# Seven quarter products in place of eight for most of an MLP's first product, in a two-layer fp32 decoder trunk on one core

## The chip, the core and the metric

The kernel runs on one core of a Trainium2 chip. A core has a matrix engine (TensorE, PE in the profile; its weight loads are PEld), VectorE (DVE), ScalarE (ACT), GpSimd (POOL) and SyncE (SP), each with an instruction queue of its own that is worked through in order, and 16 DMA engines. The metric is the device time of one execution in microseconds (us); lower is better.

## The reference

Two layers, each with a mixer and an MLP, work on 512 tokens of 1024 features, all in float32. The change touches the MLP alone:

```python
D_FF = 4 * D_MODEL      # 4096, with D_MODEL 1024, SEQ 512, DEPTH 2
h = rms_norm(x, g_pre_mlp[l]) * (1 + sc_mlp) + sh_mlp
f = jnp.square(jax.nn.relu(h @ w_ff1[l].astype(h.dtype))) @ w_ff2[l].astype(h.dtype)
x = x + gt_mlp * rms_norm(f, g_post_mlp[l])
```

`sc_mlp`, `sh_mlp` and `gt_mlp` are adaLN values: parts of `c_act @ w_ada[l] + b_ada[l]`, a product of one vector with a 1024 x 6144 matrix for each layer.

## The kernel before, in words

Activations lie with features on the 128 partitions and the 512 tokens along the free axis, so the MLP's `h` is 8 tiles of 128 x 512, its hidden layer 32 such tiles, and its result 8.

**Precision.** The matrix engine works on fp32r, so every operand is split into a high part (a cast) and a low part (what the cast lost). A product block is three passes, high by high, high by low and low by high (`passes`, L173 to L179, the three matmul lines L177, L178 and L179). An activation pair lies in one `slot`.

**Weights.** A block of 128 output features by 1024 inputs (512 KB) comes by one DMA on SP's queue into `raw` (RAW = 4 buffers); ACT casts the high part (L169) and POOL subtracts for the low part (L170). The halves go to `whi` and `wlo`, two buffers each. A tile of a first or second product with such a block (`gemm`) is 8 times 3 matmuls of 128 x 512.

**The MLP** (L763 to L803), for each layer: `wff1` tiles 0 to 6 in two token halves of 256 (`gemm_parts`; their weights were preloaded while the mixer ended), tiles 7 to 15 at 512 tokens; then `wff2` over the first half of the hidden layer (8 result tiles, two weight blocks each); then `wff1` tiles 16 to 31; then `wff2` over the third quarter (8 tiles, one block each, added to `y` on DVE at L798); the last quarter is done in `finish`, in token halves, which also adds the residual, computes norms and starts what follows. Six of its eight blocks are split ahead of it into free slots (KF = 6). After each `wff1` tile `f_out` (L764 to L769) squares the relu: ACT relu (L766), DVE product into PSUM (L767), ACT cast to the high part (L768), DVE subtraction to the low part (L769).

**Columns.** 56 of the adaLN values' 128-row columns, most of them of layer 1, are worked out during layer 0's MLP. `ada_col` loads a 512 KB block by SP's queue into `adr` (ADR = 3 buffers) and reduces it against a broadcast vector on DVE (L272, 128 x 1024, both inputs in SBUF). `some(n)` puts n of them behind a tile: before, 1 behind each full `wff1` tile and 2 behind each `wff2` tile.

**Order.** The tile scheduler orders each engine's queue by program order and priorities; weight work stands earlier in program order than its use (`high_priority`). `mm` has three PSUM banks; `cv`, `ax` and `cx` are further banks.

Of the kernel before, what the change touches and what calls it, by code (L numbers as in the profile page):

```python
# [53 lines left out]
def trunk(ctx, tc, xT, vecs, bg, cst, ccol, crow, wadn, wadt, win, win0, wqkv, wgate, wout, wff1, wff2, yT):  # L54
# [103 lines left out]
    def wblock(src, alloc=None, lo_eng=None, pri=None):  # L158
        n = src.shape[-1]
        with tc.high_priority(offset=WPRI if pri is None else pri):  # L160
            flat = lambda t: t.rearrange("p a b -> p (a b)")
            raw = wpool.tile([P, n], F32, name="raw", tag="raw", bufs=RAW)
            if alloc is not None:
                hi, lo = flat(alloc())[:, 0:n], flat(alloc())[:, 0:n]
            else:
                hi = wpool.tile([P, n], F32, name="whi", tag="whi", bufs=WHI)
                lo = wpool.tile([P, n], F32, name="wlo", tag="wlo", bufs=WLO)
# [5 lines left out]
    def passes(out, w, col, pair, first, last, ts=slice(0, T)):  # L173
# [589 lines left out]
    def mlp(l, hp, pre):  # L763
        def f_out(o, pr, ts):  # L764
# [136 lines left out]
```

## Time and profile before

| what | before |
|---|---|
| runs (three) | 1609.31, 1610.56, 1612.74 us, median 1610.56 |
| the profiled execution | 1608.05 us, of which the span from the first to the last instruction is 1606.3 |
| PE busy | 1537.6 us (96%) |
| DVE, POOL, ACT busy | 878.1 (55%), 798.5 (50%), 688.6 us (43%) |
| chain that ended last | PE 78%, DVE 6%, ACT 2%, POOL 1% |
| mean granted TensorE clock | 0.989 |

Layer 0's MLP lies between about 480 and 830 us of the span, layer 1's between about 1245 and 1606. An engine's busy share is an average over stages; the rows below are of single stages.

### The profile page before, as it was taken

What the parts mean: (1) busy time and instruction counts of PE and PEld (TensorE: products, weight loads), DVE (VectorE), ACT (ScalarE), POOL (GpSimd) and SP (SyncE); (2) the same over time, 40 slices, a digit from 0 to 9 for tenths busy, and PEclk for the clock granted to TensorE, in tenths of its full rate; (3) what the DMA queues carried; (4) which work ended last, traced back from release to release, by engine and by line L of the source; (5) the groups of instructions that cost most, each with busy time, mean ns of one, the idle gap of its engine ahead of it and who ended that gap; (6) DMA issues with size and microseconds to landing.
All of it is one profiled execution on the core that took longest, in us unless ns stands there. A gap on an engine that the chain in (4) does not pass through costs nothing.

```text
span 1606.3 us, 21229 instructions
## 1 busy us (share of the span) xinstructions
PE 1537.6 (96%) x8020; PEld 1255.5 (78%) x8020; DVE 878.1 (55%) x1761; ACT 688.6 (43%) x1168; POOL 798.5 (50%) x488
## 2 busy tenths in 40 slices
PE   4899998999999999999999999999999999999997
PEld 3577665677998888888899777676899888888887
DVE  6399999843164432346747999997326320012114
ACT  3345563453454322332453665544355432233242
POOL 0166662256744444445962877434674444444462
PEclk9999999999999999999999999999999999999999
DMA  8514332413412555556730222220242233222331
GB/s 309 194 53 138 116 131 104 144 53 92 145 53 94 191 187 197 174 194 218 255 116 8 73 79 67 91 79 27 84 141 65 80 95 102 92 92 92 96 127 53
DMA packets 56270, 188.91 MB, mean 118 GB/s; under 512 B 6376, under 2 KB 8552, under 8 KB 56168
## 3 DMA queue, kind: packets, MB, share of 16 engines
q1 hardware_dynamic: 56168, 187.56, 35.2%
q8 instruction: 63, 1.03, 0.3%
q14 instruction: 39, 0.32, 0.1%
HBM read 185.44 MB, written 2.10 MB: 117 GB/s over the span
## 4 chain that ended last, share of the span: by engine, by line
PE 78%; DVE 6%; ACT 2%; POOL 1%; issue 1%; DMA 0%; POOLq 0%; ACTq 0%; DVEq 0%
PE ps_mm L177 23%; PE ps_mm L179 23%; PE ps_mm L178 23%; DVE ps_cv L429 3%; PE ps_mm L672 2%; PE ps_mm L660 2%; PE ps_ax L316 1%; PE ps_ax L245 1%; POOL wlo L170 1%; ACT whi L169 1%; PE ps_ax L578 1%; PE ps_ax L647 0%; DVE csb L490 0%; PE ps_ax L342 0%; PE ps_ax L701 0%
## 5 line engine op out<-in xcount | busy, mean ns | idle before, releaser
L170 POOL TENSOR_TENSOR wlo<-raw,whi 128x1024 fp32r<-128x1024 f32 (+1 forms) x216 | 498.8, 2311 | 565.1 <-ACT whi L169 547.0
L177 PE MATMUL ps_mm<-slot,whi 128*128 128x512 f32 (+1 forms) x1632 | 621.9, 382 | 8.1 <-ACT slot L155 4.9
L179 PE MATMUL ps_mm<-slot,wlo 128*128 128x512 f32 (+1 forms) x1632 | 622.1, 382 | 5.0 <-POOL wlo L170 4.8
L178 PE MATMUL ps_mm<-slot,whi 128*128 128x512 f32 (+1 forms) x1632 | 621.7, 381 | 0.0
L169 ACT CAST whi<-raw 128x1024 fp32r<-128x1024 f32 (+1 forms) x216 | 216.4, 1002 | 498.9 <-PE ps_mm L178 357.7
L177 PEld LDWEIGHTS ps_mm<-slot,whi 128*128 128x128 f32 x1632 | 307.3, 188 | 78.9 <-ACT slot L155 5.6
L179 PEld LDWEIGHTS ps_mm<-slot,wlo 128*128 128x128 f32 x1632 | 307.6, 188 | 73.8 <-issue 6.3
L178 PEld LDWEIGHTS ps_mm<-slot,whi 128*128 128x128 f32 x1632 | 308.0, 189 | 65.6 <-issue 3.8
L429 DVE SCALAR_TENSOR_TENSOR ps_cv<-slot,vv,ps_cv 128x512 f32<-128x512 f32 x480 | 332.9, 747 | 1.5
L767 DVE TENSOR_TENSOR ps_mm<-rl,ps_mm 128x512 f32<-128x512 f32 (+1 forms) x78 | 46.7, 599 | 280.6 <-ACT rl L766 280.5
L177 PE MATMUL ps_mm<-slot 128*128 128x256 f32 (+1 forms) x568 | 158.5, 292 | 14.5 <-DVE slot L769 7.4
L178 PE MATMUL ps_mm<-slot 128*128 128x256 f32 (+1 forms) x568 | 163.2, 290 | 0.3 <-POOL slot L355 0.3
L179 PE MATMUL ps_mm<-slot 128*128 128x256 f32 (+1 forms) x568 | 162.6, 289 | 0.0
L177 PEld LDWEIGHTS ps_mm<-slot 128*128 128x128 f32 x568 | 105.3, 190 | 19.9 <-ACT slot L357 8.4
L179 PEld LDWEIGHTS ps_mm<-slot 128*128 128x128 f32 x568 | 107.8, 190 | 2.2 <-issue 0.8
L178 PEld LDWEIGHTS ps_mm<-slot 128*128 128x128 f32 x568 | 107.6, 190 | 1.9 <-POOL slot L355 0.5
L170 POOL TENSOR_TENSOR slot<-raw,slot 128x1024 fp32r<-128x1024 f32 x34 | 85.2, 2527 | 14.4 <-issue 12.7
L272 DVE CUSTOM_DVE_ANT_0 adr<-adr,cbc,ini 128x1024 f32<-128x1024 f32 x40 | 66.0, 1659 | 23.3 <-DMA adr<-in_wadt 23.3
L147 POOL TENSOR_TENSOR small<-small,mhalf 128x4 f32<-128x4 f32 (+1 forms) x38 | 34.6, 911 | 81.3 <-DVE small L146 76.6
L769 DVE TENSOR_TENSOR slot<-ps_mm,slot 128x512 fp32r<-128x512 f32 (+1 forms) x78 | 46.4, 595 | 38.2 <-ACT slot L768 37.9
L530 POOL TENSOR_TENSOR xa<-xa,s 128x512 f32<-128x512 f32 x48 | 61.9, 1289 | 5.1 <-ACT s L529 1.9
L768 ACT CAST slot<-ps_mm 128x512 fp32r<-128x512 f32 (+1 forms) x78 | 39.8, 510 | 45.9 <-DVE ps_mm L767 45.9
(201 smaller groups left out, 1570.5 us busy)
## 6 DMA issues: line engine op xcount, KB each, us to landing
raw<-in_wff SPq DMA_DIRECT2D x138, 512.0 KB, 3.5
raw<-in_win SPq DMA_DIRECT2D x58, 512.0 KB, 3.3
adr<-in_wadt SPq DMA_DIRECT2D x56, 512.0 KB, 4.5
raw<-in_wout SPq DMA_DIRECT2D x36, 512.0 KB, 3.5
adr<-in_wadn SPq DMA_DIRECT2D x28, 512.0 KB, 4.2
raw<-in_wqkv SPq DMA_DIRECT2D x24, 256.0 KB, 2.6
slot<-in_wadt SPq DMA_DIRECT2D x8, 512.0 KB, 5.1
raw<-in_win SPq DMA_DIRECT2D x8, 384.0 KB, 7.1
```

The costliest lines, as they stand in the source:

```text
L147: pool.tensor_tensor(y, u, mhalf[:, 0:n], op=ALU.pow)
L169: act.copy(out=r32(hi), in_=raw)
L170: (lo_eng or pool).tensor_tensor(r32(lo), raw, hi, op=ALU.subtract)
L177: pe.matmul(out, whi, xh, start=first, stop=False)
L178: pe.matmul(out, whi, xl, start=False, stop=False)
L179: mark[0] = pe.matmul(out, wlo, xh, start=False, stop=last)
L272: red = dve.tensor_tensor_reduce(raw, raw, cbc, scale, 0.0 if one else ini, ALU.mult, ALU.add, m)
L429: dve.scalar_tensor_tensor(acc, at[i][:, k:k + T], w, acc, op0=ALU.mult, op1=ALU.add)
L530: pool.tensor_tensor(acc, acc, tk, op=ALU.add)
L767: dve.tensor_tensor(o, rl[:, ts], o, op=ALU.mult)
L768: act.copy(out=r32(pr[:, 0, ts]), in_=o)
L769: last[0] = dve.tensor_tensor(r32(pr[:, 1, ts]), o, pr[:, 0, ts], op=ALU.subtract)
```

## The change

In the first product the 32 output tiles are worked in four groups of eight. Tiles 0 to 7 stay as they were (NB = 8 in halves, where there were 7). Tiles 8 to 31 are worked in twelve pairs for each layer. A pair's 256 outputs, 1024 inputs and 512 tokens are cut into halves each, and the eight products of quarters become seven (`pair_out`: w1 to w7 are the seven combinations of weight quarters, `hp`, `ta` and `tb` the activations' combinations). A quarter product is 4 times 3 matmuls of 256 tokens, so a pair is 84 matmuls of 128 x 256 where it was 48 of 128 x 512. The activation combinations `ta` and `tb` are made once for each layer (`quarters`). The weight combinations are made for each pair: `s1` and `s2p` in PSUM (ACT copy, two DVE operations), `s3` on POOL, `s4` on DVE, seven high casts on ACT, five low subtractions on POOL and two on DVE, all 128 x 512. Results are summed on the way out of PSUM: `p1` (an ACT copy), `u2`, `q5` and three more additions on DVE, all 128 x 256, and four `f_out` of 128 x 256 instead of two of 128 x 512. Weights share one tag of four buffers.

Group g's hidden tiles feed one block of `wff2` (8 tiles, each followed by a copy to `y` or an addition); the last group's block stays in `finish`. `some` now puts 2 columns behind each `wff2` tile of group 0, 3 in group 1 and 2 in group 2; none stand behind `wff1` tiles.

```diff
-    NB = 7
+    NB = 8
-    WHI = 2
-    WLO = 2
+    WBUF = 4
...
+        def quarters():
+            for k in range(4):
+                b1, b2 = s2(), s2()
+                dve.tensor_tensor(b1, hp[k][:, 0, :], hp[k][:, 1, :], op=ALU.add)
+                dve.tensor_tensor(b2, hp[4 + k][:, 0, :], hp[4 + k][:, 1, :], op=ALU.add)
+                pa, pb = bank("ax"), bank("cx")
+                dve.tensor_tensor(pa[:, A], b1[:, B], b1[:, A], op=ALU.subtract)
+                dve.tensor_tensor(pa[:, B], b2[:, B], b1[:, B], op=ALU.subtract)
+                dve.tensor_tensor(pb[:, A], b2[:, B], pa[:, A], op=ALU.subtract)
+                dve.tensor_tensor(pb[:, B], b2[:, A], pb[:, A], op=ALU.subtract)
...
+        def pair_out(m, pm, pm1):
...
+                s1, s2p = bank("ax"), bank("cx")
+                act.copy(out=s1, in_=a21)
+                w1 = wq(a11, pool)
+                dve.tensor_tensor(s1, a22, s1, op=ALU.add)
+                dve.tensor_tensor(s2p, s1, a11, op=ALU.subtract)
+                w6 = wq(s2p, dve)
+                w2 = wq(a12, pool)
+                w5 = wq(s1, dve)
+                s3, s4 = s2(), s2()
+                pool.tensor_tensor(s3, a11, a21, op=ALU.subtract)
+                w7 = wq(s3, pool)
+                dve.tensor_tensor(s4, a12, s2p, op=ALU.subtract)
+                w3 = wq(s4, pool)
+                w4 = wq(a22, pool)
...
+            bx, ba, bb, bc = (bank(t)[:, 0:T // 2] for t in ("mm", "cv", "mm", "mm"))
+            p1, u2, q5 = sqt(), sqt(), sqt()
+            prod(bx, w1, hp[0:4], h0)
+            act.copy(out=p1, in_=bx)
+            prod(ba, w6, tb, h0)
+            dve.tensor_tensor(u2, ba, p1, op=ALU.add)
+            prod(bx, w2, hp[4:8], h0, True)
+            f_out(bx, pm, h0)
+            prod(bb, w5, ta, h0)
+            dve.tensor_tensor(q5, bb, u2, op=ALU.add)
+            prod(bc, w7, ta, h1)
+            dve.tensor_tensor(ba, bc, q5, op=ALU.add)
+            f_out(ba, pm1, h1)
+            prod(bb, w3, hp[4:8], h1, True)
...
+            prod(bc, w4, tb, h1, True)
...
-        for hf in range(2):
+        for g in range(4):
...
+                for u in range(4):
+                    fp += [slot(), slot()]
+                    pair_out(8 * g + 2 * u, fp[-2], fp[-1])
+            if g == 3:
+                break
             for m in range(NF):
-                o = gemm([wff2[l, hf, m, k] for k in range(2 - hf)], fp)
+                o = gemm([wff2[l, g // 2, m, g % 2]], fp)
...
+                some(3 if g == 1 else 2)
```

The order in which the scheduler puts this differs from program order at three places of which the prediction speaks. Lines of the changed kernel are one lower than those of the kernel before up to `mlp`.

ScalarE, layer 1, from the end of one `wff1` tile to the next, in the kernel before (L169 the high cast of a later tile's weights, L766 relu, L768 high cast of the result):

```order
L766 ACTIVATE rl<-ps_mm 128x512
L768 CAST slot<-ps_mm 128x512
L169 CAST whi<-raw 128x1024
L766 ACTIVATE rl<-ps_mm 128x512
L768 CAST slot<-ps_mm 128x512
```

The same engine in the changed kernel, layer 1, while the second pair of the second group runs (L154 the high casts of weight quarters, `s_13120` and `s_13121` being `s3` and `s4` of that pair, so the casts of w7 and w3; L826 the copy `p1`; L765 and L767 relu and cast of `f_out`):

```order
L154 CAST wq<-ps_ax 128x512
L765 ACTIVATE rl<-ps_mm 128x256
L154 CAST wq<-s_13120 128x512
L765 ACTIVATE rl<-ps_mm 128x256
L154 CAST wq<-s_13121 128x512
L826 COPY sq<-ps_mm 128x256
L767 CAST slot<-ps_mm 128x256 x2
L154 CAST wq<-raw 128x512
```

In this pair the matrix engine runs w6's product, then w1's, then w2's into w1's bank. The cast of w3 (s_13121) takes the buffer of w1, and the copy `p1` of w1's result, which must leave the bank before w2's product is added there, stands behind that cast. In the third and fourth pair of a group the copy stands ahead of it.

VectorE, layer 0, `wff2` over the third quarter in the kernel before (L798 the addition to `y`, L272 a column and the reading of its sum):

```order
L798 TENSOR_TENSOR yt<-yt,ps_mm 128x512
L272 ISA adr,mod_110<-adr,cbc,ini_112,vv 128x1024
L272 ISA mod_110 128x1
L272 ISA adr,mod_110<-adr,cbc,ini_112,vv 128x1024
L272 ISA mod_110 128x1
L798 TENSOR_TENSOR yt<-yt,ps_mm 128x512
```

VectorE in the changed kernel, layer 0, from the last addition of the second group's `wff2` on (L867 that addition, L271 a column, L155 the low part of w5, L828 `u2`, L832 `q5`, L834 the addition into `ba`, L815 `s4` of the following pair; all but the first are of the third group's first two pairs):

```order
L867 TENSOR_TENSOR yt<-yt,ps_mm 128x512
L271 ISA adr,mod_110<-adr,cbc,ini_112 128x1024
L271 ISA mod_110 128x1
L155 TENSOR_TENSOR wq<-ps_ax,wq 128x512
L271 ISA adr,mod_110<-adr,cbc,ini_112 128x1024
L271 ISA mod_110 128x1
L828 TENSOR_TENSOR sq<-ps_cv,sq 128x256
L271 ISA adr,mod_110<-adr,cbc,ini_112 128x1024
L271 ISA mod_110 128x1
L766 TENSOR_TENSOR ps_mm<-rl,ps_mm 128x256
L832 TENSOR_TENSOR sq<-ps_mm,sq 128x256
L271 ISA adr,mod_110<-adr,cbc,ini_112 128x1024
```

Two more columns follow in that pair. Six of the 24 columns of this group thus stand between the operations that bring the next pair's results out of PSUM.

SyncE's queue in layer 0's third quarter of `wff2` in the kernel before (L270 the load of a column, L168 that of a weight block):

```order
L270 DMA adr<-in_wadt 128x1024 x3
L168 DMA raw<-in_wff 128x1024
L270 DMA adr<-in_wadt 128x1024 x2
L168 DMA raw<-in_wff 128x1024
L270 DMA adr<-in_wadt 128x1024 x2
```

SyncE's queue at the place above in the changed kernel (L269 the load of a column, L801 and L802 the two weight loads of a pair, the third group's four pairs in turn; up to the end of the second group's columns):

```order
L269 DMA adr<-in_wadt 128x1024 x3
L802 DMA raw<-in_wff 128x1024
L269 DMA adr<-in_wadt 128x1024 x2
L801 DMA raw<-in_wff 128x1024
L269 DMA adr<-in_wadt 128x1024 x2
L802 DMA raw<-in_wff 128x1024
L269 DMA adr<-in_wadt 128x1024 x5
L801 DMA raw<-in_wff 128x1024
L269 DMA adr<-in_wadt 128x1024 x2
L802 DMA raw<-in_wff 128x1024
L269 DMA adr<-in_wadt 128x1024 x2
```

The last three columns of the second group are loaded behind the third pair's two weight loads, which need the `raw` buffers of the first pair; the last of them stands behind the second of these loads. In the kernel before, two or three column loads alternate with one weight block, and each block's buffer comes free with a single tile.

## Rows read from the trace of the kernel before

**Rows 1.** The page: span, busy time of each engine, the granted clock in tenths of full speed in 40 slices, and the shares of the chain that ended last by engine.

```profile
span 1606.3 us, 21229 instructions
PE 1537.6 (96%) x8020; PEld 1255.5 (78%) x8020; DVE 878.1 (55%) x1761; ACT 688.6 (43%) x1168; POOL 798.5 (50%) x488
PEclk9999999999999999999999999999999999999999
PE 78%; DVE 6%; ACT 2%; POOL 1%; issue 1%; DMA 0%; POOLq 0%; ACTq 0%; DVEq 0%
```

**Rows 2.** Busy time by stretches of the span: stretch, its length, then busy us (and instructions) of PE, PEld, DVE, ACT and POOL, granted clock, DMA share and GB/s. In turn: layer 0's full `wff1` tiles 7 to 15, first half of `wff2`, `wff1` tiles 16 to 31, third quarter of `wff2`; layer 1's first half of `wff2`, `wff1` tiles 16 to 31, and the end.

```profile
509.70:560.00 50.30, 50.30 (x219) 40.63 (x218) 22.04 (x34) 18.81 (x28) 21.78 (x10) 1.00 0.53 174
560.00:649.20 89.20, 89.20 (x386) 72.02 (x385) 23.68 (x37) 21.23 (x26) 38.81 (x16) 1.00 0.54 188
649.20:738.50 89.30, 89.30 (x386) 72.12 (x385) 39.24 (x60) 33.56 (x48) 38.50 (x16) 1.00 0.58 189
738.50:789.00 50.50, 48.35 (x210) 39.17 (x209) 43.70 (x40) 15.59 (x16) 37.78 (x13) 0.97 0.75 267
1325.00:1414.00 89.00, 89.00 (x385) 72.00 (x384) 1.39 (x2) 21.24 (x25) 38.24 (x16) 1.00 0.29 94
1414.00:1504.00 90.00, 90.00 (x390) 72.89 (x389) 20.80 (x30) 33.84 (x48) 38.58 (x16) 1.00 0.30 97
1551.00:1606.00 55.00, 45.75 (x386) 45.39 (x384) 20.95 (x56) 16.81 (x35) 14.47 (x12) 0.93 0.15 49
```

**Rows 3.** The timeline of PE (start, duration): the first and last of 31 consecutive matmuls of 128 x 512, and the first and last of 19 consecutive ones of 128 x 256.

```profile
554.83 0.39 PE L179 MATMUL ps_mm<-slot,wlo 128*128 128x512 f32 x1
...
561.80 0.39 PE L179 MATMUL ps_mm<-slot,wlo 128*128 128x512 f32 x1
489.75 0.28 PE L179 MATMUL ps_mm<-slot 128*128 128x256 f32 x1
...
491.89 0.28 PE L179 MATMUL ps_mm<-slot 128*128 128x256 f32 x1
```

**Rows 4.** The timeline of DVE and ACT in layer 1's full `wff1` tiles: DVE's first operation of two tiles in turn, and ACT's three operations of a tile; in brackets the idle time before, and what ended it.

```profile
1310.24 0.70 DVE L767 TENSOR_TENSOR ps_mm<-rl,ps_mm 128x512 f32<-128x512 f32 x1 [3.52 <-ACT rl L766]
1315.81 0.70 DVE L767 TENSOR_TENSOR ps_mm<-rl,ps_mm 128x512 f32<-128x512 f32 x1 [3.52 <-ACT rl L766]
1314.23 1.05 ACT L169 CAST whi<-raw 128x1024 fp32r<-128x1024 f32 x1 [2.67 <-PE ps_mm L178]
1315.19 0.59 ACT L766 ACTIVATE rl<-ps_mm 128x512 f32<-128x512 f32 x1
1316.54 0.59 ACT L768 CAST slot<-ps_mm 128x512 fp32r<-128x512 f32 x1 [0.76 <-DVE ps_mm L767]
```

**Rows 5.** The timeline of ACT and DVE where `f_out` works on 128 x 256 (layer 0, tiles in halves).

```profile
496.33 0.38 ACT L766 ACTIVATE rl<-ps_mm 128x256 f32<-128x256 f32 x1 [0.21 <-PE ps_mm L179]
496.62 0.37 ACT L768 CAST slot<-ps_mm 128x256 fp32r<-128x256 f32 x1
496.74 0.43 DVE L767 TENSOR_TENSOR ps_mm<-rl,ps_mm 128x256 f32<-128x256 f32 x1 [0.16 <-ACT rl L766]
497.08 0.42 DVE L769 TENSOR_TENSOR slot<-ps_mm,slot 128x256 fp32r<-128x256 f32 x1
```

**Rows 6.** POOL: two groups of the page (us busy, mean ns of one), the low part of a weight block and a 128 x 512 operation of the mixer; and the timeline of one weight block in layer 1's `finish`, its low part on POOL.

```profile
L170 POOL TENSOR_TENSOR wlo<-raw,whi 128x1024 fp32r<-128x1024 f32 (+1 forms) x216 | 498.8, 2311 | 565.1 <-ACT whi L169 547.0
L530 POOL TENSOR_TENSOR xa<-xa,s 128x512 f32<-128x512 f32 x48 | 61.9, 1289 | 5.1 <-ACT s L529 1.9
1552.59 2.40 POOL L170 TENSOR_TENSOR wlo<-raw,whi 128x1024 fp32r<-128x1024 f32 x1
```

**Rows 7.** The timeline of DVE and POOL in layer 0's third quarter of `wff2`: additions to `y`, columns, and low parts of weight blocks.

```profile
744.24 0.69 DVE L798 TENSOR_TENSOR yt<-yt,ps_mm 128x512 f32<-128x512 f32 x1 [0.94 <-PE ps_mm L179]
744.84 1.28 DVE L272 CUSTOM_DVE_ANT_0 adr<-adr,cbc,vv 128x1024 f32<-128x1024 f32 x1
746.05 3.42 DVE L272 CUSTOM_DVE_ANT_0 adr<-adr,cbc,vv 128x1024 f32<-128x1024 f32 x1
749.80 0.69 DVE L798 TENSOR_TENSOR yt<-yt,ps_mm 128x512 f32<-128x512 f32 x1 [0.33 <-PE ps_mm L179]
...
766.50 0.69 DVE L798 TENSOR_TENSOR yt<-yt,ps_mm 128x512 f32<-128x512 f32 x1 [0.25 <-PE ps_mm L179]
773.21 0.68 DVE L798 TENSOR_TENSOR yt<-yt,ps_mm 128x512 f32<-128x512 f32 x1
779.91 0.68 DVE L798 TENSOR_TENSOR yt<-yt,ps_mm 128x512 f32<-128x512 f32 x1
789.21 0.69 DVE L798 TENSOR_TENSOR yt<-yt,ps_mm 128x512 f32<-128x512 f32 x1 [2.61 <-PE ps_mm L179]
745.17 3.20 POOL L170 TENSOR_TENSOR wlo<-raw,whi 128x1024 fp32r<-128x1024 f32 x1 [3.16 <-ACT whi L169]
772.15 6.73 POOL L170 TENSOR_TENSOR slot<-raw,slot 128x1024 fp32r<-128x1024 f32 x2
```

**Rows 8.** DMA issues from 738 to 790 us (line, queue, count, KB each, median us from issue to landing).

```profile
adr<-in_wadt SPq DMA_DIRECT2D x14, 512.0 KB, 4.3
raw<-in_wff SPq DMA_DIRECT2D x11, 512.0 KB, 4.3
```

**Rows 9.** The waits from 1200 us to the end, PE's largest (us in total, times, longest).

```profile
PE ps_mm L177 <- DVE slot L769: 4.0, 2, 2.9
```

More of the change, by code (lines that the diff above doesn't have):

```diff
@@ L165, in wblock @@
             else:
-                hi = wpool.tile([P, n], F32, name="whi", tag="whi", bufs=WHI)
-                lo = wpool.tile([P, n], F32, name="wlo", tag="wlo", bufs=WLO)
+                hi = wpool.tile([P, n], F32, name="whi", tag="w", bufs=WBUF)
+                lo = wpool.tile([P, n], F32, name="wlo", tag="w", bufs=WBUF)
             sp.dma_start(out=raw, in_=src)
@@ L171, in wblock, with passes @@
         return hi, lo
-    def passes(out, w, col, pair, first, last, ts=slice(0, T)):
+    def passes(out, w, col, pair, first, last, ts=slice(0, T), more=False):
         hi, lo = w
@@ L176, in passes @@
         xh, xl = r32(pair[:, 0, ts]), r32(pair[:, 1, ts])
-        pe.matmul(out, whi, xh, start=first, stop=False)
-        pe.matmul(out, whi, xl, start=False, stop=False)
-        mark[0] = pe.matmul(out, wlo, xh, start=False, stop=last)
+        pe.matmul(out, whi, xh, start=first, stop=False, skip_group_check=more)
+        pe.matmul(out, whi, xl, start=False, stop=False, skip_group_check=more)
+        mark[0] = pe.matmul(out, wlo, xh, start=False, stop=last, skip_group_check=more)
     spare = [0]
@@ L769, in f_out @@
             last[0] = dve.tensor_tensor(r32(pr[:, 1, ts]), o, pr[:, 0, ts], op=ALU.subtract)
+        h0, h1 = half(0), half(1)
+        A, B = slice(0, T // 2), slice(T // 2, T)
+        ta, tb = [], []
+        def quarters():
[8 more added lines that the diff above has]
+                dve.tensor_tensor(pb[:, B], b2[:, A], pb[:, A], op=ALU.subtract)
+                for p_, out in ((pa, ta), (pb, tb)):
+                    pr = slot()
+                    split(pr, p_)
+                    out.append(pr)
@@ new lines, in wq, with prod @@
+        def wq(src, lo_eng):
+            t = wpool.tile([P, 2, T], F32, name="wq", tag="w", bufs=WBUF)
+            split(t, src, lo_eng=lo_eng)
+            return t
+        def pair_out(m, pm, pm1):
+            with tc.high_priority(offset=WPRI):
+                ra = wpool.tile([P, D], F32, name="raw", tag="raw", bufs=RAW)
+                rb = wpool.tile([P, D], F32, name="raw", tag="raw", bufs=RAW)
+                sp.dma_start(out=ra, in_=wff1[l, m])
+                sp.dma_start(out=rb, in_=wff1[l, m + 1])
+                a11, a12, a21, a22 = ra[:, 0:T], ra[:, T:D], rb[:, 0:T], rb[:, T:D]
+                s1, s2p = bank("ax"), bank("cx")
[12 more added lines that the diff above has]
+                w4 = wq(a22, pool)
+            def prod(out, w, bs, ts, more=False):
+                for k in range(4):
+                    passes(out, (w[:, 0, :], w[:, 1, :]), k * P, bs[k], not more and k == 0, k == 3, ts, more)
+            bx, ba, bb, bc = (bank(t)[:, 0:T // 2] for t in ("mm", "cv", "mm", "mm"))
[12 more added lines that the diff above has]
+            prod(bb, w3, hp[4:8], h1, True)
+            dve.tensor_tensor(bb, bb, u2, op=ALU.add)
+            f_out(bb, pm, h1)
+            prod(bc, w4, tb, h1, True)
+            dve.tensor_tensor(bc, bc, u2, op=ALU.add)
+            f_out(bc, pm1, h0)
@@ L771, in mlp @@
         y = None
-        for hf in range(2):
+        for g in range(4):
             fp = []
-            if hf == 0:
+            if g == 0:
                 def first_out(m, ts, o):
```

17 lines of the change are left out of this document (4 added, 13 removed).

## The prediction

> **What bounds the kernel now.** I read the page first, then the stages of the two MLPs. [...] In layer 1 PE's largest wait is 4.0 us in all, at the start of the tiles in halves [rows 9]. So matmul time that is taken out of the MLP shortens the run, as long as the other engines keep pace with what takes its place.
>
> Two prices of PE decide the gain. Consecutive matmuls of 128 x 512 start (561.80 - 554.83) / 30 = 0.2323 us apart, those of 128 x 256 (491.89 - 489.75) / 18 = 0.1189 us apart [rows 3]: half the columns cost 51% of the time. Full tiles follow each other every 1315.81 - 1310.24 = 5.57 us [rows 4], 24 times 0.2321.
>
> **What the change removes, adds and moves.**
>
> PE: a pair was 48 x 0.2323 = 11.15 us and becomes 84 x 0.1189 = 9.99; 24 pairs in two layers give 24 x 1.162 = 27.9 us. The eighth tile in halves costs 24 x (2 x 0.1189 - 0.2323) = 0.13 us, twice, 0.3. `wff2` has as many matmuls as before. PE alone: -27.6.
>
> [...]
>
> The collision in layer 0 goes. From 744.24 to 789.21 eight additions to `y` take 44.97 us where seven steps of 5.57 are 38.99 [rows 7]: 6.0 us are lost, all from 766.50 on, where POOL has two low parts for each tile (one for a later block) and DVE two columns. A column takes 1.28 us beside an idle POOL and 3.42 beside its subtraction, and that one 3.2 instead of 2.40 [rows 6, 7]: the two shut each other out. In the changed kernel all columns are done before the last group's pairs, and the split of later blocks meets none. -6.0.
>
> The vector engines' load in a pair of 9.99 us: POOL six operations of 1.29 [rows 6], 7.7 us (77%). DVE five of 128 x 512 at 0.69 and thirteen of 128 x 256 at 0.42 [rows 5, 7], 8.9 at most. ACT eight of 128 x 512 at 0.59 and nine of 128 x 256 at 0.38 [rows 4, 5], 8.1 at most (durations overlap by some 0.1 where operations follow directly). All fit, none has much room. Every DVE operation in a pair has one input in PSUM; beside POOL's subtractions such ones kept 0.69 to 0.70 us [rows 4, 7], so I add nothing for POOL. [...]
>
> The wait on `p1`. In the second pair of each group the copy stands on ACT behind the cast of w3, which waits for the end of w1's product; PE has w2's product next, into the bank that the copy reads. PE waits for the cast (0.59) and the copy (0.38, rows 5) with their hand-overs, about 1.1 us. In the third and fourth pair another product lies between, 12 x 0.1189 = 1.43 us, which covers the copy. Six such pairs: +6.6. Bounds: 0 if PE's queue had work from elsewhere (it has none here), 24 x 1.1 = 26 if every pair paid.
>
> The start of `finish`. Its first block was split long before the stage; now its high cast stands on ACT behind the last pair's fifth result, some 1.9 us after that product's end (addition 0.42, relu 0.38, product 0.43, cast 0.37, with hand-overs), then the cast 1.05 [rows 4] and POOL's 2.40 [rows 6]. PE needs the low part 2 x 1.43 + 0.24 us after the same point: 5.35 - 3.1, about +2.2 in each layer, +4.4. After that POOL's 2.40 for each block stays under PE's 24 x 0.1189 = 2.85.
>
> The columns in layer 0. All 56 now lie behind 24 `wff2` tiles. In groups 0 and 2, two for each tile of 5.57 us: the rows from 744.24 to 766.50 show that this fits with one low part of POOL. I take +1 for each, since their last columns stand among the next pair's operations. In group 1, three for each tile: 1.28 + 3.42 + 1.28 + 0.69 = 6.7 us of DVE if one of them meets POOL [rows 7], 1.1 above the tile, up to 9 us in eight tiles; DMA would move four blocks of 0.52 MB in 5.57 us, 377 GB/s, where the fullest stretch moved 267 at 0.75 busy, so 356 at full [rows 2], +0.3 for each tile. But six of the 24 stand behind the last tile, so I take +3 (0 to 9). Those six stand in front of the next two pairs' `u2`, `q5` and low parts, and the last is loaded behind a weight load that waits for the first pair's `raw`: product 4's end, cast 0.59, low part 1.29, landing 4.3 [rows 8], column 1.28, some 7.5 us, where PE has three products and w1's of the next pair, 5.7. With the earlier ones that is 2 to 6 us; I take +4. Columns together +9 (2 to 17).
>
> `quarters` (32 DVE operations in each layer, 16 of 128 x 512 and 16 of 128 x 256, 17.8 us by the durations above) lies beside group 0's `wff2`, 44.6 us in which DVE has little but 16 columns, 21 us; +0, and up to 2 if it delays the first pair. The eight additions to `y` more per layer (0.69 each) lie beside 5.57 us tiles: 0.
>
> Sum: -27.6 - 6.0 + 6.6 + 4.4 + 9 = -13.6 us against the profiled execution's 1608.05, 1594.5. The median of the runs lies 2.5 above that execution, so I forecast **1597 us** as the median, 0.85% faster. What a measurement tells from no change is about 0.2%, 3.2 us.
>
> **The rivals.** *Nearly all of the gain arrives*: `p1` and `finish` cost half and the columns 2, 1610.6 - 33.6 + 5.5 + 2, about 1584. For it: PE's queue runs ahead and the four weight buffers give three products, 4.3 us, from a buffer's release to its need. Against it: the order shown on ACT.
>
> *The columns take most of it*: at their upper bounds (17, and 2 for `quarters`), 1607. For it: DVE and POOL shut each other out, and during pairs POOL is never long idle, so that each of the six columns waits for a 1.29 us operation and holds up the next. Against it: the same load fitted from 744 to 766.
>
> *Slower: the pair is paced by the in-order queues of ACT, DVE and POOL.* Each pair sends 8 results through ACT, DVE, ACT, DVE with hand-overs, between eight casts each of which waits for the product whose buffer it takes; a cast that waits holds up the release of a PSUM bank, and one `cv` and three `mm` banks carry all four sums. One late link for each half pair, at the price of the `p1` wait (1.1 us), is 2.2 us a pair, 24 x 2.2 - 6.6 = +46, 1643 at the most, some 1620 if it is half of that. It decides from 13.6 / 24 = 0.6 us a pair beyond the sum. For it: ACT and DVE above 80% of a pair by durations. Against it: where such a chain ran on 128 x 256, its four links took from 496.33 to 497.50, 1.2 us [rows 5], less than one product, and most casts of a pair wait for products that ended before.
>
> **How the numbers follow.** Forecast, 1589 to 1603: 0.50. Nearly all, 1575 to 1589: 0.16. Columns, 1603 to 1611: 0.16. Paced by the vector queues, above 1611: 0.18. Leaving out the best quarter of the second (0.04) and most of the last (0.13) gives 1579 to 1615. Faster by over 3.2 us (below 1607.3): 0.50 + 0.16 + half of the third, 0.74. Within: the other half, 0.08, and a little of the last, 0.10 together. Slower: 0.16.
>
> **What would show it.** PE busy some 27 us less, with 2016 matmuls of 128 x 256 at 0.119 us; third and fourth pairs 10 us apart; in second pairs a PE wait of about 1.1 us on the `p1` copy (ACT sq, L826); a wait on POOL's low part at the start of each `finish`; in layer 0 PE waits in pairs 5 and 6 (of 12) on DVE; no stretched columns after the last group's pairs begin. Wrong it would be if steady pairs are further apart than 10.6 us, or if layer 0 loses more than layer 1's gain.

## The result

The changed kernel takes 1629.18 us (median; 1623.84 to 1634.20) where the kernel before takes 1609.93: a ratio of 1.0118, 95% interval 1.0082 to 1.0154. It is 1.2% slower; the forecast was 1597 us, 0.85% faster, with 1615 as the upper end of its range. (One execution of a later run, 2503.6 us at a mean granted clock of 0.557, is left out of that run's median.) The profiled execution took 1629.53 us. Its page (span, busy time of each engine, granted clock in 40 slices, chain by engine), the counterpart of [rows 1]:

```profile
span 1627.7 us, 24038 instructions
PE 1530.2 (94%) x8932; PEld 1293.2 (79%) x8932; DVE 1059.1 (65%) x2181; ACT 773.5 (48%) x1454; POOL 879.3 (54%) x586
PEclk9999999999999999899999999999999999999998
PE 65%; DVE 12%; DMA 4%; ACT 3%; POOL 2%; issue 2%; SPq 0%; POOLq 0%; ACTq 0%; DVEq 0%
```

PE's share of the chain fell from 78 to 65%, and DVE's doubled. PE is busy only 7.4 us less than before, where 27.6 were forecast; part of the rest is clock. By the table of cores the mean granted clock is 0.980 over 1627.7 us and was 0.989 over 1606.3: 0.020 x 1627.7 = 32.6 against 0.011 x 1606.3 = 17.7 us of full clock are missing, 14.9 us more.

Where the time went is read best by stages. Busy time by stretches of the changed kernel (columns as in [rows 2]): for layer 0 the eight tiles in halves, then in turn `wff2` of group 0, the pairs of group 1, `wff2`, the pairs of group 2, `wff2`, the pairs of group 3; for layer 1 the halves and the three groups of pairs:

```profile
470.20:525.50 55.30, 46.27 (x346) 44.51 (x345) 41.20 (x93) 29.02 (x64) 22.31 (x13) 0.91 0.18 58
524.50:569.50 45.00, 44.76 (x195) 35.95 (x194) 27.95 (x37) 13.69 (x20) 21.70 (x11) 1.00 0.75 259
569.50:610.80 41.30, 40.30 (x337) 39.80 (x336) 27.41 (x64) 28.23 (x63) 29.88 (x22) 1.00 0.42 129
610.80:656.90 46.10, 45.13 (x195) 35.99 (x194) 35.82 (x47) 9.48 (x14) 22.75 (x10) 1.00 0.72 241
656.90:710.90 54.00, 45.37 (x338) 44.27 (x337) 42.11 (x83) 29.00 (x63) 35.10 (x23) 0.91 0.55 184
710.90:755.90 45.00, 44.72 (x194) 35.93 (x193) 36.20 (x46) 9.39 (x14) 23.85 (x9) 1.00 0.69 226
755.90:802.60 46.70, 43.37 (x337) 41.59 (x335) 33.64 (x69) 27.35 (x63) 29.91 (x22) 0.96 0.35 109
1253.20:1308.20 55.00, 46.46 (x345) 44.65 (x344) 40.80 (x93) 29.07 (x65) 21.63 (x13) 0.91 0.20 58
1352.10:1393.70 41.60, 40.38 (x337) 39.87 (x336) 26.13 (x60) 28.29 (x63) 29.35 (x22) 1.00 0.33 102
1438.40:1480.00 41.60, 40.38 (x338) 39.88 (x337) 26.76 (x61) 27.83 (x62) 29.12 (x22) 1.00 0.32 102
1524.70:1567.30 42.60, 40.54 (x338) 39.84 (x336) 27.26 (x62) 27.08 (x62) 26.92 (x21) 1.00 0.33 100
```

The same first stage in the kernel before, seven tiles in halves and the first full one, in layer 0 and in layer 1:

```profile
469.90:516.30 46.40, 42.29 (x323) 40.06 (x323) 21.57 (x59) 22.90 (x54) 18.64 (x12) 1.00 0.22 68
1234.60:1281.80 47.20, 42.40 (x323) 40.11 (x323) 22.02 (x59) 23.18 (x54) 18.65 (x12) 1.00 0.23 68
```

Four pairs took the place of eight full tiles, 44.6 us. In layer 1 they take 41.6, 41.6 and 42.6: the saving is there, 8 us of the layer. But the stage in halves, where I had put nothing but 0.1 us, is 8.9 and 7.8 us longer, and layer 0's groups 2 and 3 take 54.0 and 46.7. From the first stage's end to the first addition of `finish`, layer 0 takes 6.6 us more than before (282.5 for 275.9) and layer 1 4.9 less (264.6 for 269.4); the rest of the run is 2.9 longer. Of this rest 2.7 lie between the two MLPs, from layer 0's first addition of `finish` to layer 1's first `f_out`: 442.4 us before, 445.1 here. The work there is the same in every kernel below, and in their traces it takes 443.8 to 451.0; so a few us between two whole traces decide little, and what an edit did is read from the stages that it touches.

**The stage in halves.** PE, DVE and POOL there (layer 0, timelines; DVE L779 to L782 belong to `quarters`, L357 is the low part of the second token half of `h`, L768 the low part in `f_out`):

```profile
490.68 1.12 DVE L779 TENSOR_TENSOR s<-slot 128x512 f32<-128x512 f32 x1
492.44 2.17 DVE L780 TENSOR_TENSOR s<-slot 128x512 f32<-128x512 f32 x1
494.53 1.22 DVE L779 TENSOR_TENSOR s<-slot 128x512 f32<-128x512 f32 x1
496.01 2.23 DVE L782 TENSOR_TENSOR ps_ax<-s 128x256 f32<-128x256 f32 x1
498.16 0.86 DVE L357 SCALAR_TENSOR_TENSOR slot<-ps_cv,mod,slot 128x256 fp32r<-128x256 f32 x2
499.94 0.68 DVE L780 TENSOR_TENSOR s<-slot 128x512 f32<-128x512 f32 x1
491.21 2.85 POOL L169 TENSOR_TENSOR wlo<-raw,whi 128x1024 fp32r<-128x1024 f32 x1
495.16 2.79 POOL L169 TENSOR_TENSOR wlo<-raw,whi 128x1024 fp32r<-128x1024 f32 x1
498.68 0.39 PE L177 MATMUL ps_mm<-slot 128*128 128x256 f32 x1 [3.33 <-DVE slot L357]
501.61 0.58 PE L176 MATMUL ps_mm<-slot 128*128 128x256 f32 x1 [1.62 <-DVE slot L768]
```

The scheduler had put the combinations into DVE's queue as soon as their inputs were ready, ahead of the last pieces of `h` and of `f_out`. Two of them met POOL's subtraction and took 2.2 us where such an operation takes 0.68 alone (499.94; 0.42 for the short one). PE stood for 3.3 and 1.6 us. The granted clock of the stage is 0.91: 0.09 x 55.3 = 5.0 us of full clock are missing. Some 1.7 of these, by the clock of 0.66 from 475 to 480, went before the combinations had begun; most of the rest went with the two stops (0.50 from 500 to 505, 0.85 from 505 to 510).

**Layer 0's group 2.** The last additions to `y` (L867) and the columns (L271) on DVE at the end of the second group's `wff2`, and PE's waits after it:

```profile
652.61 0.68 DVE L867 TENSOR_TENSOR yt<-yt,ps_mm 128x512 f32<-128x512 f32 x1
656.11 0.68 DVE L867 TENSOR_TENSOR yt<-yt,ps_mm 128x512 f32<-128x512 f32 x1
656.71 1.33 DVE L271 CUSTOM_DVE_ANT_0 adr<-adr,cbc,ini 128x1024 f32<-128x1024 f32 x1
659.77 1.76 DVE L271 CUSTOM_DVE_ANT_0 adr<-adr,cbc,ini 128x1024 f32<-128x1024 f32 x1
662.07 1.67 DVE L271 CUSTOM_DVE_ANT_0 adr<-adr,cbc,ini 128x1024 f32<-128x1024 f32 x1
663.67 0.68 DVE L867 TENSOR_TENSOR yt<-yt,ps_mm 128x512 f32<-128x512 f32 x1
664.49 0.55 PE L176 MATMUL ps_mm<-slot,wq 128*128 128x256 f32 x1 [4.10 <-DVE yt L867]
679.63 0.38 PE L176 MATMUL ps_mm<-slot,wq 128*128 128x256 f32 x1 [1.59 <-ACT sq L826]
683.55 0.38 PE L176 MATMUL ps_mm<-slot,wq 128*128 128x256 f32 x1 [2.24 <-DVE slot L768]
```

The last addition came at 663.67, behind these three columns (4.8 us) and four operations of the pairs; PE had been through with `wff2` and the pair's first two products since 660.4. Until the addition is done its PSUM bank is not free for another result of the pair. PE stood for 4.1 us, the granted clock was 0.50 from 665 to 670, and two more stops followed. In the last group, whose pairs begin at 755.9, two stretched columns stand beside the first pair as well:

```profile
761.20 2.39 DVE L271 CUSTOM_DVE_ANT_0 adr<-adr,cbc,ini 128x1024 f32<-128x1024 f32 x1
763.52 2.29 DVE L271 CUSTOM_DVE_ANT_0 adr<-adr,cbc,ini 128x1024 f32<-128x1024 f32 x1
```

### The profile page after: what moved, and what is told of

It reads as the page before. It is cut to its first block, busy times and chain, and to the rows that moved or that the text cites. A ratio compares the mean times of both kernels' runs of the same rounds, so it can differ in the third digit from the quotient of the medians.

```text
span 1627.7 us, 24038 instructions
## 1 busy us (share of the span) xinstructions
PE 1530.2 (94%) x8932; PEld 1293.2 (79%) x8932; DVE 1059.1 (65%) x2181; ACT 773.5 (48%) x1454; POOL 879.3 (54%) x586
## 4 chain that ended last, share of the span: by engine, by line
PE 65%; DVE 12%; DMA 4%; ACT 3%; POOL 2%; issue 2%; SPq 0%; POOLq 0%; ACTq 0%; DVEq 0%
PE ps_mm L176 19%; PE ps_mm L178 19%; PE ps_mm L177 19%; DMA raw<-in_wff 3%; DVE adr L271 3%; DVE ps_cv L428 2%; PE ps_mm L659 2%; PE ps_mm L671 1%; POOL wq L155 1%; PE ps_ax L315 1%; PE ps_ax L244 1%; DMA adr<-in_wadt 1%; POOL wlo L169 1%; PE ps_ax L577 1%; DVE ps_ax L807 1%
## 5 line engine op out<-in xcount | busy, mean ns | idle before, releaser
L169 POOL TENSOR_TENSOR wlo<-raw,whi 128x1024 fp32r<-128x1024 f32 (+1 forms) x170 | 389.6, 2294 | 381.9 <-ACT whi L168 357.6
L176 PE MATMUL ps_mm<-slot,whi 128*128 128x512 f32 (+1 forms) x1264 | 472.5, 375 | 8.2 <-ACT slot L154 4.9
L178 PE MATMUL ps_mm<-slot,wlo 128*128 128x512 f32 (+1 forms) x1264 | 472.6, 375 | 5.0 <-POOL wlo L169 4.8
L177 PE MATMUL ps_mm<-slot,whi 128*128 128x512 f32 (+1 forms) x1264 | 472.4, 374 | 0.2 <-POOL slot L155 0.2
L168 ACT CAST whi<-raw 128x1024 fp32r<-128x1024 f32 (+1 forms) x170 | 168.0, 988 | 329.7 <-PE ps_mm L177 227.8
L176 PEld LDWEIGHTS ps_mm<-slot,whi 128*128 128x128 f32 x1264 | 238.1, 188 | 60.8 <-ACT slot L154 5.6
L178 PEld LDWEIGHTS ps_mm<-slot,wlo 128*128 128x128 f32 x1264 | 238.3, 189 | 58.4 <-POOL wlo L169 8.5
L177 PEld LDWEIGHTS ps_mm<-slot,whi 128*128 128x128 f32 x1264 | 238.4, 189 | 47.9 <-issue 3.8
L176 PE MATMUL ps_mm<-slot 128*128 128x256 f32 (+1 forms) x568 | 162.7, 297 | 20.0 <-DVE slot L768 13.3
L176 PE MATMUL ps_mm<-slot,wq 128*128 128x256 f32 x576 | 166.0, 289 | 16.2 <-ACT sq L826 7.4
L177 PE MATMUL ps_mm<-slot 128*128 128x256 f32 (+1 forms) x568 | 166.7, 295 | 6.1 <-DVE slot L357 5.3
L178 PE MATMUL ps_mm<-slot 128*128 128x256 f32 (+1 forms) x568 | 166.0, 294 | 0.0
L177 PE MATMUL ps_mm<-slot,wq 128*128 128x256 f32 x576 | 163.3, 285 | 0.0
L178 PE MATMUL ps_mm<-slot,wq 128*128 128x256 f32 x576 | 161.0, 285 | 0.5 <-DVE wq L155 0.5
L155 POOL TENSOR_TENSOR wq<-raw,wq 128x512 fp32r<-128x512 f32 x72 | 96.5, 1341 | 57.4 <-ACT wq L154 56.2
L176 PEld LDWEIGHTS ps_mm<-slot,wq 128*128 128x128 f32 x576 | 110.8, 192 | 20.2 <-ACT sq L826 10.2
L177 PEld LDWEIGHTS ps_mm<-slot,wq 128*128 128x128 f32 x576 | 111.1, 193 | 0.3
L178 PEld LDWEIGHTS ps_mm<-slot,wq 128*128 128x128 f32 x576 | 110.0, 194 | 0.8 <-DVE wq L155 0.8
```

The costliest lines, as they stand in the source:

```text
L155: (lo_eng or dve).tensor_tensor(lo, src, pair[:, 0, :], op=ALU.subtract)
L176: pe.matmul(out, whi, xh, start=first, stop=False, skip_group_check=more)
L177: pe.matmul(out, whi, xl, start=False, stop=False, skip_group_check=more)
L178: mark[0] = pe.matmul(out, wlo, xh, start=False, stop=last, skip_group_check=more)
```

## The experiments

All kernels were run beside the kernel before; ratios are to it.

**The combinations late** (whole computation): their first additions are held behind the last `f_out` of the halves.

```diff
-                dve.tensor_tensor(b1, hp[k][:, 0, :], hp[k][:, 1, :], op=ALU.add)
+                behind(dve.tensor_tensor(b1, hp[k][:, 0, :], hp[k][:, 1, :], op=ALU.add), last[0])
```

(and the same for `b2`.)

> Undoes one thing of the changed kernel: the order of the activation combinations. Their first additions stand on VectorE behind the last f_out of the tiles in halves; the rest is as changed (1629.2 us). Theory A (the combinations stand on VectorE between the second token half of h and its consumers, shut POOL out, stop the matrix engine there and let its clock fall): both layers' stage in halves loses its 8 to 9 us again, so about 1629 - 17 = 1612 us. Rival B (that stage is longer because of the eighth tile, whose weights are split twice on ACT and POOL): 1627 to 1631 us, and the waits of the matrix engine in that stage stay.

Measured: 1627.8 us, ratio 1.0113 (1.0089 to 1.0137); theory A wanted 1612. Its stages in layer 0, the halves, `wff2` of group 0 and the pairs of group 1:

```profile
469.40:517.00 47.60, 43.52 (x345) 42.27 (x344) 22.58 (x61) 24.88 (x57) 21.06 (x13) 0.96 0.23 67
515.90:565.30 49.40, 45.54 (x194) 35.67 (x193) 47.30 (x63) 17.20 (x27) 23.36 (x10) 1.00 0.58 198
565.30:610.70 45.40, 41.15 (x337) 40.14 (x336) 32.83 (x70) 28.64 (x64) 32.43 (x23) 1.00 0.47 157
```

The halves come down by 7.7 us, so rival B, the eighth tile, is out for the stage itself. But in layer 0 the next two stages are 4.4 and 4.1 longer: there DVE is busy for 47.30 of 49.4 us with combinations and 16 columns. In layer 1, without columns, the halves come down by 6.6 us to 48.4 and little is given back (middle 266.0 us for 264.6). The stretch between the MLPs, which the edit does not touch, is some 3 us longer in this trace. So the whole run could not tell; the test without columns is the one with layer 1 alone, below.

**Short columns** (the reductions take 8 of 1024 elements, at the start of the program too).

```diff
-        red = dve.tensor_tensor_reduce(raw, raw, cbc, scale,
+        red = dve.tensor_tensor_reduce(raw[:, 0:8], raw[:, 0:8], cbc[:, 0:8], scale,
```

> The changed kernel with the columns' reductions over 8 of 1024 elements; all loads, their order and waits stay (leaves out most of the adaLN columns' sum). Theory C (layer 0's second and third group lose time because the columns hold VectorE, and shut out POOL, ahead of the additions to y and of the pairs' results): about 15 to 18 us less, 1611 to 1614 us, and third-group pairs of layer 0 about 10.3 us apart. Rival D (their loads, 0.5 MB each in SyncE's queue between the weight loads, make the weights late): 1624 to 1629 us, pairs as before.

**Columns without loads**: the reduction reads the broadcast vector twice, the load is left out.

```diff
-        sp.dma_start(out=raw, in_=wadt[l, c])
+        if alloc is not None:
+            sp.dma_start(out=raw, in_=wadt[l, c])
...
-        red = dve.tensor_tensor_reduce(raw, raw, cbc, scale,
+        red = dve.tensor_tensor_reduce(raw, raw if alloc is not None else cbc, cbc, scale if alloc is not None else 1e-6,
```

> The changed kernel with the columns of the MLP reduced over a block that lies in SBUF already: none of their 56 loads, all their VectorE time (leaves out the adaLN matrix in these columns). Theory C (VectorE's time and the lock with POOL): 4 us less at most, 1625 to 1629 us. Rival D (the loads): 1611 to 1616 us. If both have a share, the two runs' gains add up to more than 18 us between them only if the waits overlap.

Measured: short columns 1609.6 us, ratio 0.9994 (0.9979 to 1.0010); without loads 1626.8, ratio 1.0104 (1.0083 to 1.0125). The changed kernel gets 19.6 us faster with the reductions cut and 2.4 with the loads gone: theory C, DVE's time, and not D. Of the 19.6 some 4 lie before the MLP, since the first `f_out` comes at 466.1 us for 470.2 (the eight early columns are short as well), so the MLP's share is about 15.5; by the traces layer 0's middle part comes down by 14.2, from 282.5 to 268.3. Layer 0's groups of pairs with short columns:

```profile
565.40:606.90 41.50, 40.38 (x338) 39.87 (x337) 26.03 (x60) 28.36 (x64) 29.18 (x22) 1.00 0.40 127
651.50:696.30 44.80, 41.61 (x338) 40.04 (x336) 32.83 (x77) 29.18 (x65) 30.46 (x24) 1.00 0.55 190
740.90:782.80 41.90, 40.51 (x337) 39.79 (x335) 28.62 (x67) 27.25 (x62) 26.97 (x21) 1.00 0.33 102
```

54.0 and 46.7 became 44.8 and 41.9. Without loads the second stayed at 51.0. How much of a column's price is its longer time beside POOL's subtraction (3.42 us for 1.28 in [rows 7]) and how much its place in DVE's queue, the two runs do not say; a reduction that does not read two SBUF operands was not tried.

**Ordinary tiles in the four groups**: `pair_out` replaced by two `gemm` tiles, no combinations.

```diff
-                quarters()
...
-                    pair_out(8 * g + 2 * u, fp[-2], fp[-1])
+                    for j in range(2):
+                        o = gemm([wff1[l, 8 * g + 2 * u + j]], hp)
+                        f_out(o, fp[j - 2], slice(0, T))
```

> The changed kernel without the seven products: the pairs are two ordinary tiles of 24 matmuls of 128 x 512 and the combinations are not made; four groups, eight tiles in halves, shared weight buffers and the columns 2, 3, 2 behind each tile stay. Theory A and C: no loss in the stage in halves; the matrix engine has 28 us more than the changed kernel; columns still late in layer 0's second group but without pairs to hold up. 1629 - 17 + 28 - 7 (no wait on p1) - 10 = 1623 us or less, down to 1612. Rival B: the halves keep their loss, 1635 us or more.

Measured: 1632.5 us, ratio 1.0138 (1.0118 to 1.0158), above both theories' figures of 1623 and near B's 1635, but not for B's reason: its stage in halves is 47.6 us long in layer 0 and 46.8 in layer 1, near the 46.4 and 47.2 before. So the regrouping alone, without the seven products, comes out 22 us slower than the kernel before. Its trace is 23.7 longer, of which 15.1 lie behind the halves of the two MLPs: layer 0's middle part takes 282.2 us for 275.9, and layer 1's 278.3 for 269.4. The last of these is largely the start of `finish`, where the first result comes 6.7 us later than one tile after the previous stage; PE waits 3.0 us there for the first block's high part (ACT, L168). Another 8.6 lie between the MLPs (451.0 us for 442.4); the mean granted clock of the whole trace is 0.984 for 0.989, and why this stretch is longer stays open. The seven products as changed have a median 3 us lower, which the two intervals do not tell apart.

**`p1` first**: the copy gets a higher priority and stands ahead of the cast of w3.

```diff
-            act.copy(out=p1, in_=bx)
+            with tc.high_priority(offset=4 * WPRI):
+                act.copy(out=p1, in_=bx)
```

> The changed kernel with one thing moved: the copy p1 goes ahead of the cast of w3 on ScalarE in each group's second pair (a higher priority for the copy). Theory E (the waits on p1 cost about 1 us in each second pair, as the trace of the changed kernel shows, 7.4 us in ten waits): 1629 - 6 = 1623 us. Rival F (ScalarE's queue is what paces these pairs, so that the cast of w3, now later, makes w3's product wait instead): 1627 to 1631 us.

Measured: 1624.7 us, ratio 1.0088 (1.0073 to 1.0103), 4.4 us less than the changed kernel. PE's waits on the copy in layer 1's pairs, the changed kernel's and then this one's (us in total, times, longest):

```profile
PE ps_mm L176 <- ACT sq L826: 4.5, 6, 1.0
```

```profile
PE ps_mm L176 <- ACT sq L827: 2.2, 4, 0.8
```

Theory E holds: over both layers the waits on the copy went from 7.4 to 3.0 us. The two medians' intervals overlap, but the six groups of pairs, stage by stage, are 4.3 us shorter in all.

**All three moves**: combinations late, `p1` first, columns spread (none behind the first three tiles of group 0's `wff2` nor behind the last tile of the other groups, 14 behind pairs).

```diff
-                some(3 if g == 1 else 2)
+                some((0 if m < 3 else 2) if g == 0 else (3, 3, 2, 2, 2, 2, 2, 0)[m])
...
+                    some(2 if g > 1 and u == 1 else 1)
```

> The changed kernel with three things moved: the activation combinations behind the last f_out of the tiles in halves, the copy p1 first, and the columns spread: none behind the first three wff2 tiles of group 0 and none behind the last of the others, 3 or 2 behind the rest, and 14 of them behind pairs. All work is done. Theory A and C together: 15 us back in the halves, 6 of p1, 10 to 14 of the columns, so about 1629 - 33 = 1596 us, faster than the kernel before. Rival G (VectorE's total in layer 0's MLP does not fit beside the matrix engine's, wherever it stands): layer 0 keeps its loss, 1612 us or more.

**The same two moves with short columns** (those of the MLP alone, where the changed kernel has them):

```diff
+        w = D if alloc is not None else 8
-        red = dve.tensor_tensor_reduce(raw, raw, cbc, scale,
+        red = dve.tensor_tensor_reduce(raw[:, 0:w], raw[:, 0:w], cbc[:, 0:w], scale,
```

> As the run with the three moves, but the columns where the changed kernel has them, and those of the MLP reduced over 8 of 1024 elements (leaves out most of these columns' sum; loads stay). It shows what the seven products give when neither the combinations nor p1 nor the columns stand in the way. Theory A and C: 1629 - 15 - 15 - 6 = 1593 us or less; 11 to 12 us gained in each layer against the kernel before, apart from its columns. Rival F and G (the pairs themselves are paced by the vector engines): 1605 us or more.

Measured: all three moves 1611.2 us, ratio 1.0009 (0.9996 to 1.0022): 18 us back, no better than the kernel before, and near rival G's 1612. Its pair groups in layer 0 take 43.1, 46.1 and 46.3 us, those of layer 1 40.7, 40.6 and 42.5. With short columns 1598.1, ratio 0.9919 (0.9900 to 0.9938), between the theories' figures. The two differ by 13 us: spread out like this, the columns cost about as much as where the changed kernel has them.

**Layer 1 alone**: the seven products, the combinations late and `p1` first in layer 1; layer 0's MLP as in the kernel before. And the same with the combinations early.

```diff
+        if l == 0:
+            return mlp0(l, hp, pre, f_out)
```

(`mlp0` is the MLP of the kernel before, NB = 7.)

> The seven products in layer 1 alone, with the combinations late and p1 first; layer 0's MLP as in the kernel before (weights in the shared buffers). Layer 1 has no columns. Theory A and E: layer 1 is 13.9 us of matmuls shorter, less 2 for the start of finish and 1 for the halves, so 1611 - 11 = 1600 us. Rival F (layer 1's pairs are paced by ScalarE and POOL): within 4 us of the kernel before, 1607 to 1614 us.

> The kernel with the seven products in layer 1 alone, but with layer 1's combinations where the changed kernel has them (not held behind the tiles in halves). Theory A (the combinations in the stage in halves stop the matrix engine there, and layer 1 has nothing that takes the gain back when they are late): 1601.5 + 6.5 = 1608 us, with the matrix engine waiting on the second half of h. Rival B: 1601 to 1603 us.

Measured: late 1601.6 us, ratio 0.9942 (0.9925 to 0.9959); early 1607.3, ratio 0.9978 (0.9964 to 0.9992). Layer 1's stage in halves, early and then late:

```profile
1235.80:1291.00 55.20, 46.63 (x345) 44.82 (x344) 40.77 (x93) 29.08 (x64) 21.63 (x13) 0.91 0.20 58
```

```profile
1238.60:1286.70 48.10, 43.78 (x345) 42.34 (x345) 22.56 (x61) 24.45 (x56) 21.07 (x13) 0.96 0.20 67
```

One move of one layer's combinations, 5.7 us of the run and 7.1 of this stage: theory A is shown where no columns stand on DVE. In the early version PE waits 2.0 us there for the second half of `h` (L357) and 5.2 in two waits for `f_out`; in the late one the first wait is gone and the others come to 3.6. The pair groups of the late version, beside 44.6 of eight full tiles:

```profile
1331.30:1372.50 41.20, 40.56 (x338) 39.92 (x337) 26.02 (x60) 28.31 (x63) 29.19 (x22) 1.00 0.34 103
1417.00:1457.60 40.60, 40.14 (x337) 39.80 (x336) 26.74 (x61) 27.89 (x62) 29.25 (x22) 1.00 0.32 105
1502.20:1543.10 40.90, 40.33 (x337) 39.75 (x335) 27.18 (x62) 27.01 (x62) 26.77 (x21) 1.00 0.33 104
```

336 matmuls at 0.1189 are 39.95. PE, not a vector engine, paces these pairs.

**`finish` of layer 1**: as layer 1 alone, with the first block through the ordinary weight buffers ahead of the preloaded ones.

```diff
-                w = kept.get(m) or wblock(blocks[m])
+                w = once.pop(m, None) or kept.get(m) or wblock(blocks[m])
...
+            once[0] = wblock(blocks[0])
+            kept = {m + 1: wblock(blocks[m + 1], a) for m, a in enumerate(allocs)}
```

> The kernel with the seven products in layer 1 alone, with one thing changed in layer 1's last stage: its first weight block goes through the ordinary weight buffers ahead of the preloaded ones (and is split again for the second token half). Theory H (the start of finish costs about 2 us because the block's high and low part come only after the last pair's results): 1601.5 - 2 = 1599.5 us. Rival: no change, 1601 to 1603 us, since the wait goes to the second block.

Measured: 1599.65 us, ratio 0.9930 (0.9911 to 0.9947), 1.9 us less, as theory H had it. The two medians' intervals overlap; the traces show the same place: PE goes from the last pair into `finish` without a stop, where layer 1 alone has one of 1.8 us, and from the pairs' last relu to the end of the span it takes 57.1 us for 59.4. It is the fastest kernel with the whole computation here: 0.7% faster than the kernel before.

**Half of layer 0 too**: groups 2 and 3 of layer 0 in pairs, group 1 in ordinary tiles that carry the combinations and 8 columns; layer 1 as in layer 1 alone. Then the same with short columns.

```diff
+            elif g == 1 and l == 0:
+                for m in range(8, 16):
+                    o = gemm([wff1[l, m]], hp)
...
+                    if m % 2:
+                        quarters([m // 2 - 4])
+                    some(1)
...
-                some(3 if g == 1 else 2)
+                some((3, 3, 2, 2, 2, 2, 2, 0)[m])
```

> A version that should beat both kernels: the seven products in all three groups of layer 1 and in groups 2 and 3 of layer 0; layer 0's group 1 is eight ordinary tiles, which carry the combinations (one set behind every second tile) and 8 columns; the other 48 columns stand behind wff2 tiles, none behind the last; p1 first, combinations in layer 1 late. Theory A and C: 8 pairs of layer 0 give 9.3 us of matmuls and the 6 us of the old collision, less 2 for finish and 2 for the halves, on top of the 8.6 us that layer 1 alone gave: 1610 - 20 = 1590 us. Rival G (layer 0's VectorE and POOL stay too full): 1600 us or more, no better than layer 1 alone (1601.5).

> The version with ordinary tiles in layer 0's group 1 and the seven products elsewhere, which came to 1604 us, with the MLP's columns reduced over 8 of 1024 elements (leaves out most of these columns' sum; all loads stay). In that version layer 0's groups of four pairs took 43.0 and 41.7 us and its wff2 groups up to 46.2, where layer 1's took 40.9 and 44.6. Theory C (what is left of the loss is still the columns on VectorE): layer 0's groups come to 41 and 44.6 us, 1604 - 8 = 1596 us. Rival J (the rest is the start of finish and the first pair of each group, whatever the columns do): 1600 us or more, pair groups 42 us or more.

Measured: 1604.05 us, ratio 0.9969 (0.9953 to 0.9984), no gain over layer 1 alone; with short columns 1597.6, ratio 0.9914 (0.9884 to 0.9944). Layer 0's pairs of group 2, `wff2` and pairs of group 3, first with the full columns, then with short ones:

```profile
652.20:695.20 43.00, 40.61 (x337) 39.84 (x336) 30.40 (x69) 28.10 (x63) 30.43 (x23) 1.00 0.43 138
695.20:741.40 46.20, 45.09 (x194) 35.95 (x193) 36.42 (x47) 9.47 (x14) 23.59 (x10) 1.00 0.70 239
741.40:783.20 41.80, 41.15 (x338) 39.91 (x337) 30.48 (x68) 27.84 (x63) 28.54 (x22) 1.00 0.34 102
```

```profile
653.00:693.90 40.90, 40.20 (x337) 39.79 (x336) 26.71 (x61) 27.78 (x62) 29.20 (x22) 1.00 0.34 108
693.90:738.50 44.60, 44.60 (x195) 36.11 (x194) 24.78 (x52) 10.13 (x15) 20.65 (x10) 1.00 0.69 247
738.50:779.00 40.50, 40.04 (x338) 39.64 (x336) 27.41 (x63) 27.16 (x62) 26.77 (x21) 1.00 0.35 105
```

The three stages are 5.0 us shorter and reach layer 1's values. Theory C again: with these columns on DVE, as placed in the runs here, layer 0 hands back what the pairs save.

## Why the prediction was wrong

The sign was wrong, and two steps of the sum made it so. Between the sum (13.6 us faster) and the two traces (21.4 slower by their spans) lie 35.0 us; beyond what the sum had in each place, 16.5 are in the two stages in halves, 12.0 in layer 0's middle part, 3.6 in layer 1's and 2.7 between the MLPs.

1. **"`quarters` ... lies beside group 0's `wff2` ...; +0, and up to 2."** This step failed. I placed the 32 operations by their place in the program. DVE's queue in the changed kernel has them among the tiles in halves, which became 8.9 and 7.8 us longer; moved behind, they gave back 7.7 and 6.6 of these. Layer 1 alone shows 5.7 us of the run for this. For the pairs the prediction had noted that every DVE operation has one input in PSUM, and so added nothing for POOL; the combinations' first additions have both inputs in SBUF (2.17 us beside POOL's subtraction for 0.68 alone), and this was not weighed. Even in the place that I had given them they were not free in layer 0, where they met the columns (49.4 and 45.4 us for 45.0 and 41.3).

2. **The columns, "+9 (2 to 17)".** The mechanism was right, a DVE that falls behind in group 1's `wff2` and columns ahead of the next pair's results, and the place as well: groups 2 and 3 of layer 0. The size was not, though it lies inside the bounds: 14 to 15.5 us, since stretches at half clock, which no term of the sum held, went with the stops of PE (0.91 and 0.96 in these two groups, 0.09 x 54.0 + 0.04 x 46.7 = 6.7 us). The "-6.0" rested on all columns being done before the last group's pairs. They were not; two ran after those pairs had begun, and stretched (2.39 and 2.29 us for 1.28). So the cost of the columns has moved to the pairs.

3. **PE, "a pair ... becomes 84 x 0.1189 = 9.99", -27.6.** Right for the matmuls: 336 of them in 40.6 us where little else stands in the way, where the rows' 0.1189 gives 39.95; so their ratio of 0.51 held. In the changed kernel layer 1's groups save 3.0, 3.0 and 2.0 us of the 4.6 each, mostly because of step 4 (4.5 of the 5.9 us that are lacking).

4. **The wait on `p1`, +6.6.** Right in kind and nearly in size: 7.4 us in ten waits, in layer 1 4.5 in six with 1.0 the longest. By the pair groups 4.3 us came back when the copy was moved, and 3.0 us of waits were left.

5. **The start of `finish`, +2.2 a layer.** Right: from the last pair's end to the first addition layer 1 takes 5.4 us where one tile is 2.85, and in the run that mended it a stop of 1.8 us is gone there, and the median is 1.9 lower.

6. **The rivals.** Slower was forecast by another road, pairs paced by the in-order queues. That did not happen; in layer 1, without columns, pairs are 10.4 to 10.7 us apart on the mean in the changed kernel, 10.2 to 10.3 with the two moves. "The columns take most of it" was nearest. None of them had the clock in it, nor the combinations at more than 2 us. Of the two signs of being wrong the second came: with its halves, layer 0's MLP became 15.5 us longer, and layer 1's 3.0 longer too.

## What to carry over

Before an added block of vector work is priced at nothing, look for it in the engine's own queue of the changed program, not in the program's text: work that is ready early is put early, in front of what the bottleneck waits for. Where the matrix engine holds the bound, a stop can have two prices, the wait and a stretch at half clock that goes with it: here the stops of 3.3 and 4.1 us had both, those of 1.0 us on the `p1` copy only the first (clock 1.00 in layer 1's groups). Sums need both. And a saving that rests on the bottleneck being fed pays only in stages whose other engines have room: here the seven products gain 0.6 to 0.7% of the run in the layer without columns and nothing, as placed in these runs, in the one with them.

## What was not expected of the hardware

With stops of 3.3 and 1.6 us, and with one of 4.1 us, rows by 5 us of the changed kernel show a granted clock of 0.50, the lower of the two levels, 1.00 and 0.50, in its trace (columns as in [rows 2]):

```profile
500.00:505.00 5.00, 3.39 (x16) 3.39 (x17) 5.00 (x13) 2.19 (x5) 0.00 (x0) 0.50 0.17 68
665.00:670.00 5.00, 5.00 (x26) 5.00 (x25) 4.64 (x9) 0.90 (x2) 1.40 (x1) 0.50 0.96 339
```

A stage with such stops came to 0.91. The kernel before and the changed kernel also have a wait of 2.9 us at the start of each stage in halves, and so has layer 0 with the combinations late. Behind it the clock stays at 1.00 in both layers of the kernel before, but falls in both of the changed kernel (0.66 from 475 to 480, 0.72 from 1258 to 1263) and in layer 0 with the combinations late (0.77 from 475 to 480). So the same stop is followed by a fall in one execution and not in another; why stays open.

A 128 x 512 addition of two SBUF operands on DVE, 0.68 us alone, took 2.17 beside POOL's subtraction, and a 128 x 256 one (0.42 alone) 2.23, while the subtraction took 2.79 and 2.85 where it takes 2.40. The one that started at 492.44, with POOL's under way since 491.21, ended at 494.61, 0.55 us after POOL's; the short one, started at 496.01 with POOL's under way since 495.16, ended at 498.24, 0.29 us after POOL's.
